# Eight experts of a group worked on from one on-chip set of token rows, selected and combined by one-hot matmuls

## The chip, the cores and the metric

The kernel runs on one core of a Trainium2 chip. The metric is the device time of one execution in microseconds (us); lower is better. TensorE is called PE here, VectorE DVE, ScalarE ACT, GpSimd POOL; SP is the sync engine, whose queue issues most of the transfers.

## The reference

One layer of a diffusion backbone over 1024 tokens of width 1024, all in fp32: a mixer (mLSTM and Hyena branches, merged), then a mixture of 64 experts in 8 groups of 8, then a final RMSNorm. Only the expert part bears on the change:

```python
glog = xt @ w_group + b_group                 # 8 groups, top 1
gsel = argmax(glog); gw = softmax(glog)[gsel]
elog = (xt @ w_router + b_router)[group gsel] # 8 experts of that group, top 2
weights = gw * topv / sum(topv)
expert(x) = (silu(x @ w1_e) * (x @ w3_e)) @ w2_e      # 1024 -> 512 -> 1024
h2 = rmsnorm(x, g_norm2) * (1 + mod4) + mod3
x = x + mod5 * sum over the two experts of weights * expert(h2)
out = rmsnorm(x, g_final)
```

Both experts of a token belong to one group. For the inputs used here the routing, worked out from the reference, gives 102 to 177 tokens to a group and at most 62 to an expert.

## The kernel before

The program is one long straight line per engine, put into order by a scheduler that sees all the dependences; within one engine instructions run in that order. The mixer takes the first 1590 us or so. Its last part (`merge`) writes each finished token row to a DRAM tensor `xg` (row and its 1/rms) and again to a DRAM tensor `xd`, the residual stream. `route` then ranks each token within its expert by matmuls with triangular ones and builds a table: 128 slots by 32 columns, column j holding 64 slots for expert j and 64 for expert j+32 (`idx` the token of a slot, `sw` its share). Slots that no token fills have an index out of bounds, and the gather skips them.

`experts` (line 1728) runs 32 iterations, j = 0 to 31, one pair of experts each. In iteration j:

- `gather` (line 1656) brings the 128 slot rows of iteration j+2 from `xg` into one of two `xs` buffers, by an indirect DMA on POOL's queue;
- `expert_up` (line 1681) multiplies `xT` with w1 and w3 of both experts: 32 matmuls of 64 columns by 512 rows, the two experts side by side in the PE array (column tiles 0 and 64), into two PSUM buffers `psz`; then silu on ACT and the product on DVE (`hm`);
- `prepare` (line 1661) makes `xT` of iteration j+1: eight 128x128 matmuls with the diagonal `dg` of 1/rms, which transpose and scale at once, and then the modulation, half on DVE and half on ACT;
- `expert_mid` (line 1695) transposes `hm` (four matmuls, line 1700) and copies the result to `hmT`;
- `expert_down` (line 1705) multiplies with w2 (16 matmuls), scales by share and `mod5` on DVE, and issues an indirect DMA that adds the 128 rows onto `xd` in DRAM.

An fp32 matmul is two instructions in the trace. PSUM holds three `psz` buffers and five `psx` buffers, taken in turn; a matmul into a `psx` buffer waits until the user of five allocations earlier is done.

The weights come through SP's queue in tiles of 1 MB (`wtile`, line 1625), 12 tiles for one pair, into a ring of NW = 19 buffers; a transfer waits for its buffer and for the fourth transfer before it. After j = 12 comes a loop (`more`, line 1799) for tokens beyond 64 of an expert; with these inputs it runs zero times, but the engines meet at its head. At the end `final_load` reads `xd` back, and `final` normalises and writes the output; the last pair's rows are added on chip and written after that (`renew`).

```python
for j in range(32):
    if j + 2 < 32:
        self.gather(xs[j % 2], ix[j + 2], P)
    ...
    hm = self.expert_up(mp, xT, W, P)
    if j < 31:
        xT = self.prepare(mp, xs[(j + 1) % 2], P)
    hT = self.expert_mid(mp, hm, P)
    ...
    add = self.expert_down(mp, hT, W, ix[j], sw[:, j:j + 1], P, acc=acc)
```

Of the kernel before, what the change touches and what calls it, by code (L numbers as in the profile page):

```python
# [9 lines left out]
F32 = mybir.dt.float32  # L10
# [27 lines left out]
NW, NA = 19, 12  # L38
# [60 lines left out]
class Body:  # L99
# [1162 lines left out]
    def merge_begin(self):  # L1262
# [3 lines left out]
        self.gp = self.kst.enter_context(self.pool("mgd", 3, side="right"))  # L1266
# [7 lines left out]
    def merge(self):  # L1274
        nc, I = self.nc, self.I
        mm = nc.tensor.matmul
        self.xd = self.dram.tile([S, D], F32, name="xd")
# [4 lines left out]
        with ExitStack() as st:  # L1282
# [6 lines left out]
            for half in range(2):  # L1289
# [41 lines left out]
                def post(t, c, ps):  # L1331
# [65 lines left out]
    def route(self, rt, hf):  # L1397

        nc = self.nc
# [6 lines left out]
        if hf == 0:  # L1406
# [5 lines left out]
            self.wt, self.rk, self.eid = kt("wt", 2, 8), kt("rk", 2, 8), kt("eid", 2, 8)  # L1412
            self.seen, self.tab0 = keep.tile([P, 64], F32R, name="seen"), kt("tab0", 96)
            ts(self.seen, self.iota[:, 0:64], 0.0, None, ALU.mult)
# [5 lines left out]
        def first_max(nm, v):  # L1420

            mx, oh, km = new(nm + "m", 4), new(nm + "o", 4, 8), new(nm + "k", 4)
# [5 lines left out]
            return mx, oh  # L1428

        gl = lg[:, :, 0:8]  # L1430
        gm, goh = first_max("g", gl)
# [6 lines left out]
        es = new("es", 4, 8)  # L1438
        red(es, sel)
        e1, oh1 = first_max("e1", es)  # L1440
        es2 = new("es2", 4, 8)
        stt(es2, oh1, -3.0e38, es, ALU.mult, ALU.add)
        e2, oh2 = first_max("e2", es2)

        f32r = lambda nm, *m: rt.tile([P, *m], F32R, name=nm)
# [4 lines left out]
        A = f32r("A", 4, 64)  # L1450
        tt(A, OH[:, 0], OH[:, 1], ALU.add)
# [3 lines left out]
        mm(pr[:, 0:256], self.sr[:, 1], self.seen.unsqueeze(1).broadcast_to([P, 4, 64]), start=True, stop=False)  # L1455
        mm(pr[:, 0:256], self.sr[:, 0], A, start=False, stop=False)
        for t in range(3):
            mm(pr[:, 64 * (t + 1):256], self.sr[:, 1], A[:, t:t + 1].broadcast_to([P, 3 - t, 64]), start=False,
               stop=(t == 2))
        odd, either, ohv = new("odd", 2, 4), new("either", 2, 4, 32), f32r("ohv", 2, 4, 32)  # L1460
        red(odd, OH[:, :, :, 32:64])
        for k in range(2):
            tt(either[:, k], OH[:, k, :, 0:32], OH[:, k, :, 32:64], ALU.add)
            tt(ohv[:, k], either[:, k], self.val[:, T].unsqueeze(2).broadcast_to([P, 4, 32]), ALU.mult)
        ohw = f32r("ohw", 2, 4, 2, 32)

        def weights():

            gw, r, w = new("gw", 4), new("r", 4), new("w", 4)
# [393 lines left out]
```

## Time and profile before

| | us |
|---|---|
| three runs, median (lowest to highest) | 2667.94 (2666.43 to 2678.24) |
| the profiled execution, its own time | 2671.49 |
| its span, first to last instruction | 2669.7 |
| PE busy (matmul) | 2486.4 (93%) |
| PE weight loads, beside the matmuls | 1675.9 (63%) |
| DVE busy | 1244.5 (47%) |
| ACT busy | 842.4 (32%) |
| mean granted PE clock | 0.971 |
| moved by DMA | 628.62 MB |

The profile shows one execution. The time of an execution is its span and 1.8 us around it. A row of the timeline is one or several instructions of one line in a row on one engine: start, length, engine, line, what it writes and reads, count, and in brackets how long the engine had waited and for what. PE is busy nearly everywhere, which by itself does not say that it sets the time; the windows and the timeline of the expert stage, from about 1625 us on, have to be read for that.

### The profile page before, as it was taken

How to read it: one execution, taken by the hardware profiler on the slowest of the kernel's cores; microseconds unless marked ns; L12 is line 12 of the kernel's file. 1: busy time of each engine (PE TensorE's matmuls, PEld its weight loads, DVE VectorE, ACT ScalarE, POOL GpSimd, SP SyncE). 2: the span in 40 equal slices, each digit the busy share in tenths (PEclk: the TensorE clock that was granted, in tenths of full speed). 3: DMA queues.
4: the chain of work that ended last, by engine and by line, in shares of the span. 5: the costliest groups of instructions: out<-in, count | busy, mean ns of one | idle time of the engine just before them, and what ended most of it. 6: DMA issues, size and time to landing. Idle time of an engine off the chain costs nothing. (4 is left out here: it accounts for less than half of the span.)

```text
span 2669.7 us, 31257 instructions
## 1 busy us (share of the span) xinstructions
PE 2486.4 (93%) x11726; PEld 1675.9 (63%) x11726; DVE 1244.5 (47%) x2845; ACT 842.4 (32%) x1606; POOL 212.5 (8%) x303
## 2 busy tenths in 40 slices
PE   7999999999999999999989997999888988898885
PEld 3777788888887888888868774444333333333332
DVE  5687868888842338766764533411111111111113
ACT  5454444554533346666343321100000000000001
POOL 1000000000010111011021010100000000000001
PEclk9999999999999999999999998999998999999997
DMA  7565532212252332233464579999998999999998
GB/s 270 157 192 159 167 126 73 73 57 81 72 148 65 110 83 84 67 99 119 161 220 148 169 245 373 412 405 400 407 403 335 412 405 394 396 396 397 401 406 330
DMA packets 236836, 628.62 MB, mean 235 GB/s; under 512 B 23514, under 2 KB 138696, under 8 KB 187532
## 3 DMA queue, kind: packets, MB, share of 16 engines
q1 hardware_dynamic: 195904, 522.49, 52.0%
q0 software_dynamic: 28800, 82.11, 9.8%
q10 hardware_dynamic: 11980, 22.01, 2.3%
q8 instruction: 93, 1.52, 0.2%
q14 instruction: 59, 0.48, 0.1%
HBM read 577.92 MB, written 65.68 MB: 241 GB/s over the span
## 5 line engine op out<-in xcount | busy, mean ns | idle before, releaser
L1688 PE MATMUL psz<-we,xT 128*64 128x512 f32 x2048 | 519.6, 618 | 56.0 <-DMA we<-in_w_e_dram 47.1
L1688 PEld LDWEIGHTS psz<-we,xT 128*64 128x64 f32 x2048 | 174.9, 142 | 354.8 <-issue 277.1
L1716 PE MATMUL psx<-we,hmT 128*64 128x512 f32 x1024 | 290.2, 614 | 24.1 <-issue 20.8
L107 DVE TENSOR_TENSOR hm<-hm,psz 128x512 f32<-128x512 f32 x32 | 22.0, 688 | 469.0 <-PE psz L1688 469.0
L122 ACT ACTIVATE xT<-psx,shp,gsp 128x128 f32<-128x128 f32 x128 | 55.4, 455 | 524.0 <-DVE xT L116 520.5
L697 PE MATMUL psz<-h0h,wh 128*128 128x512 f32 x512 | 204.0, 399 | 1.3 <-ACT h0h L122 1.3
L699 PE MATMUL psz<-h0h,wl 128*128 128x512 f32 x512 | 202.9, 396 | 0.8 <-DVE wl L535 0.8
L698 PE MATMUL psz<-h0l,wh 128*128 128x512 f32 x512 | 201.9, 394 | 0.6 <-DVE h0l L637 0.6
L699 PE MATMUL psz<-h1h,wl 128*128 128x512 f32 x512 | 201.0, 393 | 0.0
L697 PE MATMUL psz<-h1h,wh 128*128 128x512 f32 x512 | 200.5, 393 | 0.0
L698 PE MATMUL psz<-h1l,wh 128*128 128x512 f32 x512 | 200.3, 392 | 0.0
L1716 PEld LDWEIGHTS psx<-we,hmT 128*64 128x64 f32 x1024 | 88.7, 139 | 176.7 <-issue 166.0
L535 DVE TENSOR_TENSOR wl<-w,wh 128x1024 fp32r<-128x1024 f32 x104 | 127.0, 1222 | 148.4 <-ACT wh L534 124.4
L534 ACT CAST wh<-w 128x1024 fp32r<-128x1024 f32 x104 | 109.2, 1050 | 186.5 <-PE psz L698 167.2
L1670 PEld LDWEIGHTS psx<-dg,xs 128*128 128x128 f32 x512 | 124.9, 334 | 40.6 <-issue 34.8
L122 ACT ACTIVATE hm<-psz 128x512 f32<-128x512 f32 x32 | 19.1, 597 | 415.4 <-PE psz L1688 372.4
L1670 PE MATMUL psx<-dg,xs 128*128 128x128 f32 x512 | 132.2, 413 | 5.6 <-DVE dg L114 5.6
L116 DVE TENSOR_SCALAR xT<-psx,gsp,shp 128x128 f32<-128x128 f32 x128 | 49.8, 408 | 181.8 <-PE psx L1670 178.4
L110 DVE SCALAR_TENSOR_TENSOR yo<-psx,tab,m 128x512 f32<-128x512 f32 x64 | 48.0, 751 | 169.0 <-PE psx L1716 168.7
L697 PEld LDWEIGHTS psz<-h0h,wh 128*128 128x128 f32 x512 | 96.7, 189 | 26.5 <-issue 7.3
L699 PEld LDWEIGHTS psz<-h0h,wl 128*128 128x128 f32 x512 | 96.9, 189 | 23.8 <-issue 3.6
L698 PEld LDWEIGHTS psz<-h1l,wh 128*128 128x128 f32 x512 | 96.1, 188 | 22.1 <-issue 2.0
(570 smaller groups left out, 4665.4 us busy)
## 6 DMA issues: line engine op xcount, KB each, us to landing
we<-in_w_e_dram SPq DMA_DIRECT2D x366, 1024.0 KB
w<-in_w_in_dram SPq DMA_DIRECT2D x72, 512.0 KB
wm<-in_w_mod_dram SPq DMA_DIRECT2D x48, 512.0 KB
we<-in_w_e_dram SPq DMA_DIRECT2D x36, 512.0 KB
kd<-Ks ACTq DMA_DIRECT2D x8, 1088.0 KB
Kf<-kd SPq DMA_DIRECT2D x8, 1088.0 KB
gd<-sg ACTq DMA_DIRECT2D x32, 256.0 KB
w<-in_w_b_dram SPq DMA_DIRECT2D x16, 512.0 KB
```

What stands on the lines that cost most here:

```text
L107: (eng or self.nc.vector).tensor_tensor(out=out, in0=a, in1=b, op=op)
L110: self.nc.vector.scalar_tensor_tensor(out=out, in0=a, scalar=s, in1=b, op0=op0, op1=op1)
L116: self.nc.vector.tensor_scalar(out=out, in0=a, scalar1=s1, scalar2=s2, op0=op0, op1=op1)
L122: self.nc.scalar.activation(out=out, in_=in_, func=func, bias=bias, scale=scale, **kw)
L534: self.nc.scalar.copy(out=hi, in_=src)
L535: d = self.nc.vector.tensor_tensor(out=lo, in0=src, in1=hi, op=ALU.subtract)
L697: mm(ps, wh, xh, start=(k == 0), stop=False)
L698: mm(ps, wh, xl, start=False, stop=False)
L699: mm(ps, wl, xh, start=False, stop=(k == n - 1))
L1670: self.nc.tensor.matmul(pt[:, k * P:k * P + n], xs[:n, kk:D:8], dg[:n, :n], start=True, stop=True)
L1688: self.nc.tensor.matmul(ph[i][r, :], xT[:, k, r], w[i](k), start=(k == 0), stop=(k == 7), tile_position=(0, 64 * e))
L1716: nc.tensor.matmul(py[r, :], hT[:, k, r], w[2](k)[:, c * 512:(c + 1) * 512], start=(k == 0), stop=(k == 3), tile_position=(0, 64 * e))
```

## The change

The pair of iteration j becomes experts 2j and 2j+1, so that four iterations in a row (j = 4g to 4g+3) are the eight experts of group g. `route` ranks each token also within its group and builds a table of 256 rows for each group. `gather_group` fetches the rows of a group once, 2 x 128 of them, into `xs[g % 2]`; `normalize_group` scales them by 1/rms on ACT into `xn`. `prepare` picks the 128 slot rows of an iteration out of the group's 256 by a one-hot matrix `sel` in place of the diagonal: two matmuls (a = 0 and 1) where there was one. `expert_down` no longer adds to DRAM: the scaled result is split into `yh` and `yl` (fp32r), and `combine` adds it onto the group's rows on chip by one-hot matmuls, eight of 128x512 in each iteration, each result multiplied with `mod5` and added on DVE. After four iterations `finish` normalises the group's rows and writes them to the output by two indirect DMAs. `xd`, its copy in `merge`, the reading back at the end, `final` and `renew` go. The loop for the rest moves behind the last iteration; it takes tokens of a group beyond 256 or of an expert beyond 64, and has none with these inputs. The ring of weight buffers falls from 19 to 16, and a pool of gate tiles in `merge` from 3 to 2.

```diff
-NW, NA = 19, 12
+NW, NA = 16, 12
...
-        self.gp = self.kst.enter_context(self.pool("mgd", 3, side="right"))
+        self.gp = self.kst.enter_context(self.pool("mgd", 2, side="right"))
...
-                        nc.gpsimd.dma_start(self.xd[r, :], xv[:, t])
...
+        hi, row, g2 = new("hi", 4, tag="c4"), new("row", 4), new("g2", 4, 2, 8)
+        ts(hi, gr, 127.5, None, ALU.is_gt)
+        stt(row, hi, -128.0, gr, ALU.mult, ALU.add)
...
+        Rg = f32r("Rg", 4, P, tag="Rk")
+        tt(Rg, self.iota.unsqueeze(1).broadcast_to([P, 4, P]), row.unsqueeze(2).broadcast_to([P, 4, P]), ALU.is_equal)
...
+        for t in range(4):
+            mm(tgr, Rg[:, t], g3[:, t].rearrange("p a b -> p (a b)"), start=(t == 0), stop=(t == 3))
...
-        return self.wtile(("w1_e", "w3_e", "w2_e")[i // 2], j + 32 * (i % 2), first)
+        return self.wtile(("w1_e", "w3_e", "w2_e")[i // 2], 2 * j + i % 2, first)
...
+    def normalize_group(self, mp, g):
+
+        self.xn = mp.tile([P, 2, D], F32, name="xn")
+        for a in range(2):
+            x = self.xs[g % 2][:, a]
+            self.act(self.xn[:, a], x[:, :D], AF.Copy, scale=x[:, D:D + 1])
...
+    def prepare(self, mp, j):
+
+        g, p = divmod(j, 4)
+        sel = mp.tile([P, 2, P], F32, name="sel", bufs=2)
+        for a in range(2):
+            c = [self.cod[:, p, 16 * k + 8 * a + g:16 * k + 8 * a + g + 1] for k in range(2)]
+            self.ts(sel[:, a], self.iota, c[0], None, ALU.is_equal)
+            self.stt(sel[:, a], self.iota, c[1], sel[:, a], ALU.is_equal, ALU.add)
         xT = mp.tile([P, 8, P], F32, name="xT", bufs=2)
         for q in range(2):
             pt = self.ps()
             for k in range(4):
                 kk = 4 * q + k
-                self.nc.tensor.matmul(pt[:, k * P:k * P + n], xs[:n, kk:D:8], dg[:n, :n], start=True,
-                                      stop=True)
...
+                for a in range(2):
+                    self.nc.tensor.matmul(pt[:, k * P:(k + 1) * P], self.xn[:, a, kk:D:8], sel[:, a],
+                                          start=(a == 0), stop=(a == 1))
...
+    def combine(self, mp, j, y):
+
+        x = self.xs[j // 4 % 2]
+        st = mp.tile([P, 2, P], F32R, name="st", bufs=2)
+        for a in range(2):
+            self.ts(st[:, a], self.iota, self.row[:, a, j:j + 1], None, ALU.is_equal)
+        for a in range(2):
+            for c in range(2):
+                cs = slice(c * 512, (c + 1) * 512)
+                ps = self.ps()
+                for i in range(2):
+                    self.nc.tensor.matmul(ps, st[:, a], y[i][:, cs], start=(i == 0), stop=(i == 1))
+                self.tt(ps, ps, self.m5[:, cs], ALU.mult)
+                self.tt(x[:, a, cs], x[:, a, cs], ps, ALU.add)
+
+    def finish(self, mp, x, idx):
...
+        for a in range(n):
+            for c in range(2):
+                self.act(self.ps(), x[:, a, c * 512:(c + 1) * 512], AF.Square, accum_out=ss[:, a, c:c + 1])
+        self.tt(r, ss[:, :, 0], ss[:, :, 1], ALU.add)
+        self.rsqrt(mp, r, r, 1.0 / D)
+        for a in range(n):
+            self.stt(x[:, a, :D], x[:, a, :D], r[:, a:a + 1], self.gf, ALU.mult, ALU.mult)
+            off = bass.IndirectOffsetOnAxis(ap=idx[a], axis=0)
+            self.nc.gpsimd.indirect_dma_start(out=self.out[0], out_offset=off, in_=x[:, a, :D], in_offset=None, **OOB)
...
         for j in range(32):
-            if j + 2 < 32:
-                self.gather(xs[j % 2], ix[j + 2], P)
+            g, p = divmod(j, 4)
...
+            if p == 3 and g < 7:
+                self.normalize_group(mp, g + 1)
+            hm = self.expert_up(mp, xT, W)
+            if j > 0:
+                self.combine(mp, j - 1, y)
+                if p == 0:
+                    self.finish(mp, self.xs[(g - 1) % 2], group(g - 1))
+            if p == 0 and g < 7:
+                self.gather_group(g + 1)
             if j < 31:
-                xT = self.prepare(mp, xs[(j + 1) % 2], P)
...
+                xT = self.prepare(mp, j + 1)
+            hT = self.expert_mid(mp, hm)
+            y = [mp.tile([P, D], F32R, name=f"y{p}") for p in "hl"]
+            for c in range(2):
+                cs = slice(c * 512, (c + 1) * 512)
+                py = self.expert_down(hT, W, c)
+                self.act(y[0][:, cs], py, AF.Copy, scale=sw[:, j:j + 1])
+                self.stt(y[1][:, cs], py, sw[:, j:j + 1], y[0][:, cs], ALU.mult, ALU.subtract)
...
+        self.combine(mp, 31, y)
+        self.finish(mp, self.xs[1], group(7))
+        self.more(mp)
```

The scheduler puts the new work into an order of its own, which the diff does not tell. PE in a late iteration of the kernel before (`L1700` is `expert_mid`, `L1716` `expert_down`, `L1670` `prepare` for the next iteration, `L1688` `expert_up` of the next; counts are matmuls):

```order
L1700 MATMUL psx<-cmat,hm 128x128 x4
L1716 MATMUL psx<-we,hmT 64x512 x2
L1670 MATMUL psx<-dg,xs_14898 128x128 x8
L1716 MATMUL psx<-we,hmT 64x512 x14
L1688 MATMUL psz<-we,xT 64x512 x32
```

And in the changed kernel, within a group, from `expert_down` to the next `expert_up` (`L1760` is `expert_down`, `L1775` `combine`, `L1723` `prepare`, `L1737` `expert_up`):

```order
L1760 MATMUL psx<-we,hmT 64x512 x16
L1775 MATMUL psx<-yh,st 128x512
L1775 MATMUL psx<-yl,st 128x512
L1775 MATMUL psx<-yh,st 128x512
L1737 MATMUL psz<-we,xT 64x512
L1775 MATMUL psx<-yl,st 128x512
L1775 MATMUL psx<-yh,st 128x512
L1775 MATMUL psx<-yl,st 128x512
L1775 MATMUL psx<-yh,st 128x512
L1775 MATMUL psx<-yl,st 128x512
L1723 MATMUL psx<-sel,xn 128x128 x16
L1737 MATMUL psz<-we,xT 64x512 x31
```

The combine of an iteration stands right behind its own `expert_down`, and the prepare behind the combine, ahead of the next `expert_up` but for one matmul of it; in the kernel before, the prepare lay within `expert_down`.

At the six group boundaries j = 8, 12, ... 28 PE has one matmul of the prepare behind the combine, and the rest in the middle of `expert_up`:

```order
L1775 MATMUL psx<-yl,st 128x512
L1723 MATMUL psx<-sel,xn 128x128
L1737 MATMUL psz<-we,xT 64x512 x16
L1723 MATMUL psx<-sel,xn 128x128 x15
L1737 MATMUL psz<-we,xT 64x512 x15
```

DVE at such a boundary (`yl` is the low part of the result, `psx` times `m` and `xs` plus `psx` are the combine, from `r` on it is `finish`):

```order
L110 SCALAR_TENSOR_TENSOR yl<-psx,tab_13786,yh 128x512 x2
L107 TENSOR_TENSOR psx<-psx,m_15109 128x512
L107 TENSOR_TENSOR xs_14923<-xs_14923,psx 128x512
L107 TENSOR_TENSOR psx<-psx,m_15109 128x512 x2
L107 TENSOR_TENSOR xs_14923<-xs_14923,psx 128x512 x2
L107 TENSOR_TENSOR psx<-psx,m_15109 128x512
L114 TENSOR_SCALAR st<-cmat,rowt 128x128
L107 TENSOR_TENSOR xs_14923<-xs_14923,psx 128x512
L114 TENSOR_SCALAR st<-cmat,rowt 128x128
L107 TENSOR_TENSOR r<-ss 128x2
```

Four more `psx` buffers go to the squares of `finish` there, between those of the combine and those of the prepare, so that the prepare's first buffer is the one of the combine's fourth result.

## Rows read from the trace of the kernel before

**Rows 1.** The page, 40 slices of the span: PE busy, DMA share.
```profile
PE   7999999999999999999989997999888988898885
...
DMA  7565532212252332233464579999998999999998
```
**Rows 2.** Windows: PE, PEld, DVE, ACT, POOL busy (count), PE clock, DMA share, GB/s.
```profile
1700.00:1800.00 100.00, 95.66 (x408) 42.76 (x408) 17.90 (x40) 9.63 (x22) 9.29 (x8) 0.98 1.02 407
2200.00:2300.00 100.00, 88.80 (x359) 37.99 (x357) 13.88 (x27) 6.95 (x15) 7.88 (x6) 0.95 1.01 398
```
**Rows 3.** Timeline of PE, one iteration that waits for no weights (j = 5 to 6).
```profile
1786.16 0.75 PE L1700 MATMUL psx<-cmat,hm 128*128 128x128 f32 x4 [0.84 <-DVE hm L107]
1787.74 1.90 PE L1716 MATMUL psx<-we,hmT 128*64 128x512 f32 x4 [0.83 <-issue]
1789.58 4.08 PE L1670 MATMUL psx<-dg,xs 128*128 128x128 f32 x16
...
1800.13 14.27 PE L1688 MATMUL psz<-we,xT 128*64 128x512 f32 x61
1815.24 0.74 PE L1700 MATMUL psx<-cmat,hm 128*128 128x128 f32 x4 [0.84 <-DVE hm L107]
```
**Rows 4.** Timeline of PE, later: a wait for weights, and the last iterations.
```profile
1928.72 8.78 PE L1688 MATMUL psz<-we,xT 128*64 128x512 f32 x30 [3.07 <-DMA we<-in_w_e_dram]
...
2634.30 0.75 PE L1700 MATMUL psx<-cmat,hm 128*128 128x128 f32 x4 [0.85 <-DVE hm L107]
```
**Rows 5.** Timeline of PE, `expert_mid` of j = 0 and of j = 4.
```profile
1643.12 0.63 PE L1700 MATMUL psx<-cmat,hm 128*128 128x128 f32 x4
...
1756.13 0.75 PE L1700 MATMUL psx<-cmat,hm 128*128 128x128 f32 x4 [0.89 <-DVE hm L107]
```
**Rows 6.** DMA queues, 1700 to 2000 us: packets, MB, share of 16 engines.
```profile
q1 hardware_dynamic: 15932, 116.03, 94.3%
q0 software_dynamic: 2880, 5.10, 6.7%
```
**Rows 7.** Timeline of PE in the merge: fp32r matmuls of 128x512.
```profile
1542.29 0.40 PE L697 MATMUL psz<-wrh,Gh 128*128 128x512 f32 x1
...
1542.99 0.40 PE L697 MATMUL psz<-wrh,Gh 128*128 128x512 f32 x1
```
**Rows 8.** Groups of lines, 2200 to 2600 us: busy, mean ns | idle before.
```profile
L110 DVE SCALAR_TENSOR_TENSOR yo<-psx,tab,m 128x512 f32<-128x512 f32 x24 | 18.0, 751 | 58.9 <-PE psx L1716 58.9
...
L107 DVE TENSOR_TENSOR hm<-hm,psz 128x512 f32<-128x512 f32 x12 | 8.3, 688 | 192.7 <-PE psz L1688 192.7
L122 ACT ACTIVATE hm<-psz 128x512 f32<-128x512 f32 x12 | 7.2, 597 | 144.4 <-PE psz L1688 144.4
```
**Rows 9.** The start of the expert stage: timelines of POOL, DVE and PE.
```profile
1616.72 1.08 POOL L1658 DMA_INDIRECT xs<-xg,mgi  x1 [14.04 <-DVE tmp L1532]
...
1620.76 0.29 DVE L114 TENSOR_SCALAR dg<-cmat,xs 128x128 f32<-128x128 f32 x1 [2.78 <-DMA xs<-xg,mgi]
...
1621.11 4.21 PE L1670 MATMUL psx<-dg,xs 128*128 128x128 f32 x16 [5.59 <-DVE dg L114]
1625.24 14.01 PE L1688 MATMUL psz<-we,xT 128*64 128x512 f32 x64
```
**Rows 10.** The end: timelines of PE, ACT, DVE and POOL.
```profile
2635.83 7.14 PE L1716 MATMUL psx<-we,hmT 128*64 128x512 f32 x32 [0.79 <-DVE hmT L1702]
...
2642.18 1.28 ACT L122 ACT_TABLE_LOAD   x1
...
2650.49 1.06 ACT L122 ACTIVATE we<-we 128x1024 f32<-128x1024 f32 x1
...
2660.75 1.28 DVE L110 SCALAR_TENSOR_TENSOR we<-yo,r,we 128x1024 f32<-128x1024 f32 x1
...
2663.69 1.02 POOL L1797 DMA_INDIRECT out_dram<-we,mgi  x1 [23.21 <-DMA out_dram<-we]
```
**Rows 11.** Timeline of PE at the loop after j = 12.
```profile
2021.86 1.97 PE L1688 MATMUL psz<-we,xT 128*64 128x512 f32 x2 [8.83 <-issue]
```

More of the change, by code (lines that the diff above doesn't have):

```diff
@@ L1490, in route @@
+        rk = new("rk", 2, 4)
         red(rk, tmp)
[L1492 to L1503 removed]
@@ L1509, in route @@
+        rp, ohv = new("rp", 2, 4, tag="c8"), f32r("ohv", 2, 4, 32)
+        stt(rp, odd, 64.0, rk, ALU.mult, ALU.add)
+        stt(rp, ov.unsqueeze(1).broadcast_to([P, 2, 4]), 1000.0, rp, ALU.mult, ALU.add)
+        ts(gr, gr, 1.0, None, ALU.add)
+        for k in range(2):
+            tt(ohv[:, k], either[:, k], gr.unsqueeze(2).broadcast_to([P, 4, 32]), ALU.mult)
+        if hf == 1:
+            weights()
+        tv, tw = self.ps()[:, 0:32], self.ps()[:, 0:64]
         for k in range(2):
-            Rk = rt.tile([P, 4, P], F32R, name="Rk", bufs=1 + hf)
@@ new lines, in overflow @@
+        for t in range(8):
+            mm(pc[:, 0:8], self.sr[:, 1], A[:, t], start=(t == 0), stop=(t == 7))
+        cnt, thr, cmp, n, end, base, one = (new("cnt", 8), new("thr", 8), new("cmp", 8, 8), new("n", 8), new("end", 8),
+                                            new("base", 8), new("one", 8))
+        nc.vector.tensor_copy(out=cnt, in_=pc[:, 0:8])
+        ts(thr, self.iota[:, 0:8], 128.0, 0.5, ALU.mult, ALU.add)
+        over = lambda v, m: v.unsqueeze(2).broadcast_to([P, 8, m])
+        each = lambda v, m: v.unsqueeze(1).broadcast_to([P, 8, m])
@@ new lines, in overflow @@
+        nc.vector.tensor_copy(out=ex[:, 16:24], in_=end[:, 7:8].broadcast_to([P, 8]))
+        self.item = self.keep.tile([1, 24], I32, name="item")
+        nc.vector.tensor_copy(out=self.item, in_=ex[0:1, :])
+        rk, q, it = new("ork", 8), new("q", 8), new("it", 8)
+        tt(cmp, self.goh, pr[:, 0:64].rearrange("p (t g) -> p t g", g=8), ALU.mult)
+        red(rk, cmp)
+        ts(thr, thr, 127.0, None, ALU.add)
+        tt(cmp, over(rk, 8), each(thr, 8), ALU.is_gt)
+        red(q, cmp)
@@ new lines, in more @@
+            xT = mp.tile([P, 8, P], F32, name="xT", bufs=2)
+            for q in range(2):
+                pt = self.ps()
+                for k in range(4):
+                    nc.tensor.matmul(pt[:, k * P:(k + 1) * P], x[:, 0, 4 * q + k:D:8], dg, start=True, stop=True)
+                self.modulated(xT, q, pt)
+            for e in range(8):
+                W = [[self.wtile(nm, e0 + e) for nm in ("w1_e", "w3_e", "w2_e")]]
+                hT = self.expert_mid(mp, self.expert_up(mp, xT, W))
+                for c in range(2):
+                    cs = slice(c * 512, (c + 1) * 512)
+                    py = self.expert_down(hT, W, c)
+                    yo = mp.tile([P, 512], F32, name="yo", tag="yl")
+                    self.stt(yo, py, w[:, e:e + 1], self.m5[:, cs], ALU.mult, ALU.mult)
+                    self.tt(x[:, 0, cs], x[:, 0, cs], yo, ALU.add)
```

419 lines of the change are left out of this document (183 added, 236 removed).

## The prediction

> **What bounds the kernel now.** I read the page's slices first: from slice 25, about 1630 us on, the DMA row stands at 9 and PE at 8 or 9 [rows 1]. Both look full, so the windows come next: early in the expert stage PE is busy 95.7 of 100 us, later 88.8, while the DMA share is full in both [rows 2]. Then the timeline of PE tells what the two limits are. From j = 5 to j = 6 PE waits for no weights, and one iteration takes 1815.24 - 1786.16 = 29.08 us [rows 3]. Later it waits for weight tiles at the start of or within `expert_up` [rows 4]. From `expert_mid` of j = 4 at 1756.13 [rows 5] to that of j = 31 at 2634.30 [rows 4] lie 27 iterations in 878.2 us, 32.5 each. So the weight stream sets the pace, and PE alone would need 29.08: it has 3.4 us to spare in an iteration, no more. That is the number to hold against the change. The stream carries 12.58 MB for each pair of experts; POOL's own transfers, gathers and adds, take 6.7% of the engines beside the 94.3% of the weights [rows 6].
>
> **The change, part by part.** All times are of the profiled execution: span 2669.7, its own time 2671.49, 3.6 us above the median of the runs.
>
> *Removed from the DMA engines.* 2048 rows gathered, 2048 added (read and written), the copy `xd`, its reading back. What is left is 1024 rows gathered and 1024 written. POOL's share falls from 6.7% to a third or so. At 407 GB/s [rows 2] the weights of an iteration take 12.58 / 0.407 = 30.9 us, and about 0.26 MB of rows 0.6 more: an estimate of 31.5 us. This is worth about 1 us in an iteration while the stream sets the pace, and nothing once PE does.
>
> *Prepare, doubled.* Eight matmuls, 16 instructions, go from 1789.58 to the next start 4.0 us later (the row's length is 4.08 with the last one's drain) [rows 3], 0.25 us each. The change issues 32: +4.0 us on PE. It lay on PE's path before and does so now.
>
> *Combine, new.* Eight fp32r matmuls of 128x512. Three such follow each other in 1542.99 - 1542.29 = 0.70 us [rows 7], so 8 x 0.233 = 1.87 us.
>
> *A wait that the combine brings.* It stands right behind its own `expert_down` in PE's order, and its fourth matmul needs `yl` of the second half: 0.60 us on ACT (the silu row of the same shape) and 0.75 on DVE (the `yo` row) [rows 8], with handovers some 1.65 us after the last matmul of `expert_down`. Queued behind it are the rest of the combine, the prepare and all of the next `expert_up`. PE has three combine matmuls and one of `expert_up` to fill it: the third combine matmul can start at 0.85, ends at 1.1, and the lone `expert_up` matmul takes 0.9 (two take 1787.74 to 1789.58) [rows 3], to 2.0. The four of them would have cost 0.7 + 0.9 without the wait: 0.4 us lost. The bounds are 0 and 1.65; I take 0.4, which is built from the nearest rows.
>
> *The other waits* for `hm` (0.84) and `hmT` (0.83) [rows 3] stay. **The iteration becomes** 29.08 + 4.0 + 1.87 + 0.4 = 35.35 us on PE, above the 31.5 of the stream. PE is then the bound, and the weights are there: 16 buffers hold one and a third iterations, and a tile's buffer is free again nearly a whole iteration before its new content is used, so that the smaller ring costs nothing as long as PE is slower than the stream. Were it not, the ring's gaps would come on top of the 31.5.
>
> *Group boundaries.* At j = 8, 12, ... 28 the prepare's first matmul waits for the `psx` buffer of the combine's fourth result. DVE needs `yl` (done at 1.65) and then eight operations of 128x512 at 0.69 [rows 8]: 7.1 us behind `expert_down`, where PE would have been ready at 3.1. That is 4.0 us, six times: 24 us. Behind that matmul wait `expert_up` and all the rest. `finish` itself then runs on ACT, DVE and POOL beside `expert_up`, and the writes have a whole group's time. At j = 4 the order has half of `expert_up` ahead of this matmul, which covers it.
>
> *Small things at nothing.* `yl`, `st`, `sel` and the adds on DVE come to some 8 us more in an iteration in which DVE was busy under 5 of 32 [rows 2]. `normalize_group` is two ACT copies beside `expert_up`. The gate pool of two is covered by the 24 matmuls of a block (24 x 0.233 = 5.6 us) [rows 7]; were that too little, one DVE operation of 0.69 in some 30 blocks, 21 us.
>
> *The start.* Gather was issued at 1616.72, `expert_up` began at 1625.24 [rows 9]. Now the group's table takes about 1 us more of small DVE work, there are two gathers (1.08) and an ACT copy of 128x1024 (1.06), and the prepare costs another 4.2 [rows 9, 10]; the second prepare, ahead of `expert_mid` of j = 0, another 4.0. Together +11.4: `expert_mid` of j = 0 comes at 1643.12 + 11.4 = 1654.5 [rows 5].
>
> *The first four iterations* took 1756.13 - 1643.12 = 113.0 [rows 5]; `expert_up` and `expert_down` overlap there and cover the waits. With 4 x 5.87 they take 136.5: `expert_mid` of j = 4 at 1791.0.
>
> *j = 4 to 31:* 26 x 35.35 + 27.3 (the last has no prepare, 8.0 less) + 24 = 970.4: `expert_mid` of j = 31 at 2761.4. The meeting at the loop, 8.83 us of PE [rows 11], is gone from the middle; it was hidden in the mean of 32.5 above.
>
> *The end.* Before, 2669.7 - 2634.30 = 35.4 us. Now: `expert_mid` and `expert_down` 9.3 (0.75 + 0.8 + 7.7) [rows 4, 10]; to DVE's last add 7.1; a square on ACT 0.6 with its handover 0.3, a table load 1.28, seven small operations some 1.4, two scalings of 1.28: 13.2; the last indirect write, 6.0 from its issue to the end as before (2663.69 to 2669.7) [rows 10]; the loop's head, 8.83 less those 6.0, 2.8 [rows 11]. Together 31.3.
>
> **Sum:** 2761.4 + 31.3 = 2792.7 of span, and 1.8 around it: **2794 us**, 4.6% above the profiled execution, 4.7% above the median. This case's own range is 2771 to 2840: 0 to 1.65 for the wait in each of 27 iterations (-11 to +34), and half of the boundaries' 24 either way.
>
> **A rule weighed.** The 16 instructions of the prepare take 4.0 us, 0.25 each [rows 3]. The Trainium skill (TensorE: Matmul & The Clock Gate, Back-to-back issue gap) gives some 81 ns for a sustained matmul of 128 columns. By that the added half would cost 1.3 us and the sum would be lower by 31 x 2.7 = 84 us, an estimate of 2710. The row is of this very instruction in fp32, so it decides.
>
> **The rivals.**
> - *Cheaper prepares.* The added half might run into the time of the first half's weight loads. For it: four transposes of the same size take 0.60 to 0.63 us [rows 5], 0.15 each. Against it: the 16 stand at 0.25 each in every iteration. At 0.15 for the added ones 31 x 1.6 = 50 us less: **2745**.
> - *PSUM is emptied too slowly.* The boundary's wait could come in every iteration: each of the four combine results is read twice by DVE. Against it: within a group the prepare takes buffers that were left long before. For it: at six boundaries it must. Then 20 more iterations lose 4.0: **2874**. [...]
> - *The weights stay the bound (the other side).* If the added PE work fell into PE's waits, only the saved traffic would count: 878.2 x 0.943 = 828 for the weights and a third of POOL's share, 20, less the loop's 8.8: 839, so 39 less; +11 at the start, -4 at the end: **2639**. It decides below 839 / 27 = 31.1 us of PE in an iteration, that is if the additions cost 2.0 us and not 6.27. The prepare alone takes twice that.
> - *The parts cancel:* additions of about 3.4 us would fill the slack exactly, some **2670**. It would take prepares at half their price and a free combine.
>
> **How the numbers follow.** Forecast 0.72, PSUM in every iteration 0.12, cheaper prepares 0.05, the weights as bound 0.08, parts cancel 0.03. The range 2740 to 2874 takes in the first three and leaves out the last two. A measurement of this kernel can tell about 0.5%, 13 us, from no change. Faster 0.08, same 0.03, slower 0.89.
>
> **What would show it.** In the changed profile: `expert_mid` of one iteration to the next 35 us apart, 39 at the boundaries; 32 instructions of the prepare in 8.0 us; almost no PE wait for weights, and DMA windows below full; the granted clock near 1.00 throughout the stage. Wrong would be: an interval of 31 us with waits for weights (the stream still bounds), prepares of 5 us, or a wait for DVE ahead of the prepare in every iteration.

## The result and the profile after

| | before | after |
|---|---|---|
| median, us (four runs each) | 2669.61 | 2785.80 |
| lowest to highest | 2666.43 to 2678.24 | 2781.88 to 2788.81 |
| profiled execution: time, span | 2671.49, 2669.7 | 2784.48, 2782.7 |
| moved by POOL's own queue, MB | 82.11 | 65.03 |

The change makes the kernel slower: ratio 1.0429, 95% interval 1.0400 to 1.0458. The forecast was 2794.

The page of the changed kernel, slices, queues and two groups of instructions (busy, mean ns, idle before):

```profile
PE   7999999999999999999999969999999999999995
...
DMA  7555532121333223234734769989898988898982
...
q0 software_dynamic: 21776, 65.03, 7.1%
...
L1737 PE MATMUL psz<-we,xT 128*64 128x512 f32 x2048 | 482.4, 595 | 0.0
...
L1723 PE MATMUL psx<-sel,xn 128*128 128x128 f32 x1024 | 249.0, 401 | 13.3 <-DVE xs L107 9.9
```

The roles have changed hands [rows 1]. PE is at 9 through the expert stage, and it is DMA that drops, to 8 in many slices. `expert_up` (L1737) waits 0.0 us for anything, where it waited for weights before [rows 4]. The windows say it too, in the columns of [rows 2]: the DMA share falls below full.

```profile
2200.00:2300.00 100.00, 94.25 (x398) 48.38 (x395) 29.69 (x61) 13.88 (x24) 4.83 (x4) 0.98 0.89 360
```

One iteration on PE's timeline, against [rows 3]:

```profile
1827.77 0.75 PE L1748 MATMUL psx<-cmat,hm 128*128 128x128 f32 x4 [0.85 <-DVE hm L107]
1829.30 7.14 PE L1760 MATMUL psx<-we,hmT 128*64 128x512 f32 x32 [0.78 <-DVE hmT L1749]
1836.38 0.50 PE L1775 MATMUL psx<-yh,st 128*128 128x512 f32 x1
1837.17 0.50 PE L1775 MATMUL psx<-yl,st 128*128 128x512 f32 x1 [0.28 <-DVE yl L110]
...
1840.10 7.67 PE L1723 MATMUL psx<-sel,xn 128*128 128x128 f32 x32
1847.69 13.95 PE L1737 MATMUL psz<-we,xT 128*64 128x512 f32 x62
1862.49 0.75 PE L1748 MATMUL psx<-cmat,hm 128*128 128x128 f32 x4 [0.85 <-DVE hm L107]
```

From `expert_mid` to `expert_mid` it is 34.72 us; most intervals lie within 0.1 of 34.7. The prepare takes 1847.69 - 1840.10 = 7.59. At a group boundary (here j = 8) PE stands ahead of the prepare, and the interval is 37.11:

```profile
1905.81 0.50 PE L1775 MATMUL psx<-yh,st 128*128 128x512 f32 x1
...
1909.29 0.39 PE L1775 MATMUL psx<-yl,st 128*128 128x512 f32 x1
1911.33 0.74 PE L1723 MATMUL psx<-sel,xn 128*128 128x128 f32 x2 [1.65 <-DVE xs L107]
1912.00 7.09 PE L1737 MATMUL psz<-we,xT 128*64 128x512 f32 x32
```

Four intervals are some 1.7 us longer than their neighbours. Each has a stretch at a lower clock: `expert_down` takes 8.83 and not 7.14. The timeline, and the windows around it (PE busy, PE clock, DMA share, GB/s):

```profile
2146.35 8.83 PE L1760 MATMUL psx<-we,hmT 128*64 128x512 f32 x32 [0.78 <-DVE hmT L1749]
```
```profile
2110.00:2144.00 34.00, 32.78 (x140) 1.00 0.89 362
2144.00:2148.00 4.00, 2.40 (x10) 0.85 1.02 422
2148.00:2152.00 4.00, 4.00 (x15) 0.73 1.01 414
2152.00:2181.00 29.00, 28.09 (x120) 1.00 0.81 327
```

At the start DVE waits for a small DMA that the forecast did not have, and at the end the last scaling runs to 2765.0 (timeline of DVE). That DMA is issued by POOL, which at the end issues its second write late (timeline of POOL):

```profile
1610.66 0.61 DVE L107 TENSOR_TENSOR sel<-lg,goh 128x256 f32<-128x256 f32 x1 [5.67 <-DMA xg<-rb]
...
2762.51 2.48 DVE L110 SCALAR_TENSOR_TENSOR xs<-xs,r,gf 128x1024 f32<-128x1024 f32 x2
```
```profile
1603.77 0.77 POOL L1392 DMA_DIRECT2D xg<-rb  x1 [2.48 <-DVE rb L1391]
...
2764.07 1.77 POOL L1792 DMA_INDIRECT out_dram<-xs,mgi  x1 [122.91 <-DVE xs L110]
2769.62 0.97 POOL L1792 DMA_INDIRECT out_dram<-xs,mgi  x1 [3.78 <-issue]
```

### The profile page after: what moved, and what is told of

It reads as the page before. It is cut to its first block, busy times and chain, and to the rows that moved or that the text cites. A ratio compares the mean times of both kernels' runs of the same rounds, so it can differ in the third digit from the quotient of the medians.

```text
span 2782.7 us, 33165 instructions
## 1 busy us (share of the span) xinstructions
PE 2632.8 (95%) x12493; PEld 1823.7 (66%) x12493; DVE 1443.7 (52%) x3312; ACT 935.2 (34%) x1747; POOL 159.8 (6%) x254
## 3 DMA queue, kind: packets, MB, share of 16 engines
q0 software_dynamic: 21776, 65.03, 7.1%
## 5 line engine op out<-in xcount | busy, mean ns | idle before, releaser
L1737 PE MATMUL psz<-we,xT 128*64 128x512 f32 x2048 | 482.4, 595 | 0.0
L1737 PEld LDWEIGHTS psz<-we,xT 128*64 128x64 f32 x2048 | 150.8, 137 | 284.3 <-issue 278.2
L1723 PEld LDWEIGHTS psx<-sel,xn 128*128 128x128 f32 x1024 | 246.9, 334 | 24.4 <-DVE xs L107 12.5
L1723 PE MATMUL psx<-sel,xn 128*128 128x128 f32 x1024 | 249.0, 401 | 13.3 <-DVE xs L107 9.9
L1760 PE MATMUL psx<-we,hmT 128*64 128x512 f32 x1024 | 236.7, 611 | 22.8 <-DVE hmT L1749 22.0
L122 ACT ACTIVATE yh<-psx,tab 128x512 fp32r<-128x512 f32 x64 | 44.0, 687 | 444.7 <-PE psx L1760 441.9
L1760 PEld LDWEIGHTS psx<-we,hmT 128*64 128x64 f32 x1024 | 86.6, 139 | 150.8 <-issue 121.0
L110 DVE SCALAR_TENSOR_TENSOR yl<-psx,tab,yh 128x512 fp32r<-128x512 f32 x64 | 48.1, 751 | 232.1 <-ACT yh L122 229.6
```

What stands on the lines that cost most here:

```text
L110: self.nc.vector.scalar_tensor_tensor(out=out, in0=a, scalar=s, in1=b, op0=op0, op1=op1)
L122: self.nc.scalar.activation(out=out, in_=in_, func=func, bias=bias, scale=scale, **kw)
L1723: self.nc.tensor.matmul(pt[:, k * P:(k + 1) * P], self.xn[:, a, kk:D:8], sel[:, a], start=(a == 0), stop=(a == 1))
L1737: self.nc.tensor.matmul(ph[i][r, :], xT[:, k, r], w[i](k), start=(k == 0), stop=(k == 7), **kw)
L1760: self.nc.tensor.matmul(py[r, :], hT[:, k, r], w[2](k)[:, c * 512:(c + 1) * 512], start=(k == 0), stop=(k == 3), **kw)
```

## The experiments

The theory: an iteration lasts as long as the longer of two things, PE's instructions with its waits or the weight stream. The rivals: DVE empties PSUM too slowly; the smaller ring costs; PE's waits and not its instructions cost. All times are medians; the ratios are to the kernel before, run beside it on the same chip. Differences between runs set medians of different chips side by side; the kernel before took 2669.6 to 2673.6 us on them.

**1. Half of the prepare** (changed kernel; rows 128 to 255 of a group left out)

```diff
-                for a in range(2):
-                    self.nc.tensor.matmul(pt[:, k * P:(k + 1) * P], self.xn[:, a, kk:D:8], sel[:, a],
-                                          start=(a == 0), stop=(a == 1))
+                self.nc.tensor.matmul(pt[:, k * P:(k + 1) * P], self.xn[:, 0, kk:D:8], sel[:, 0],
+                                      start=True, stop=True)
```

> The second matmul of each pair in the prepare is gone (the rows 128 to 255 of a group's tile are left out of the expert inputs): 16 instructions fewer in each of 32 prepares, 0.237 us each by the changed kernel's own trace, 3.8 us. My theory (PE's own instructions set the 34.7 us of a regular iteration): PE alone falls to 30.9 us, just under the 31.5 that I estimated for the weight stream, so the stream takes over: waits for weights come back at expert_up, an iteration takes 31.5 to 32.0, and the time is about 2690 us (2665 if PE stays the bound at 30.9). Rival 1 (DVE empties PSUM too slowly): PE waits for DVE in place of the removed instructions, the gain stays below 30 us, 2756 or more. Rival 2 (the added matmuls were half hidden, as the cheaper prepares of the prediction): gain of 50 us, 2736.

Measured: 2660.70 us, ratio 0.9968 (0.9956 to 0.9979), 125 us below the changed kernel. PE's timeline, and a window of all engines:

```profile
1974.28 3.85 PE L1722 MATMUL psx<-sel,xn 128*128 128x128 f32 x16
1978.06 13.95 PE L1736 MATMUL psz<-we,xT 128*64 128x512 f32 x62
1992.86 0.75 PE L1747 MATMUL psx<-cmat,hm 128*128 128x128 f32 x4 [0.85 <-DVE hm L107]
```
```profile
2200.00:2300.00 100.00, 92.62 (x397) 41.58 (x398) 38.61 (x85) 20.65 (x38) 4.83 (x4) 1.00 1.00 409
```

An iteration takes 30.9 us, nearly all of them alike: 3.8 less, the price of 16 instructions in full. Both rivals fall. PE still sets the pace, with no wait for weights in its timeline, while the DMA share is at 1.00. With its boundary of 33.3 a group takes 31.5 in the mean, so the stream is no slower than my 31.5; whether it is faster, this run does not show. The doubled half of the prepare makes up the whole loss of the change.

**2. The combine without `yl`** (changed kernel; the low parts left out)

```diff
-                for i in range(2):
-                    self.nc.tensor.matmul(ps, st[:, a], y[i][:, cs], start=(i == 0), stop=(i == 1))
+                self.nc.tensor.matmul(ps, st[:, a], y[0][:, cs], start=True, stop=True)
...
-                self.stt(y[1][:, cs], py, sw[:, j:j + 1], y[0][:, cs], ALU.mult, ALU.subtract)
```

> The combine takes only the high part yh (yl and its four matmuls are left out, so the result has the lower precision of one rounded part). My theory: four matmuls of 0.233 us and the wait of 0.28 us for yl are gone, 1.2 us in 31 iterations, 37 us: about 2749 us. Rival 1 (what costs is the wait at the combine and not its matmuls): 0.3 us in an iteration, 2777 us. Rival 2 (DVE's work on PSUM sets the pace): DVE loses its two operations for yl, 2 x 0.75 us, and an iteration falls by 1.5 us or more, 2740 us, and a regular iteration shows waits for DVE ahead of the prepare in the kernel as it is, which I have not seen.

Measured: 2766.80 us, ratio 1.0362 (1.0345 to 1.0379), 19 us less and not 37. A regular interval falls to 33.84, by 0.87: four matmuls at 0.22. The wait stays: 0.34 us, now for `yh`. The intervals at the boundaries grew to 37.6 to 39.1, most of them 4.1 above their neighbours where it was 2.4, and took back part of the gain: each of the six has a stretch at a lower clock (0.96 over the interval of 37.97, 1.00 over its neighbours), which costs some 1.7 us; in the changed kernel one boundary has it. The price of the matmuls is confirmed; the wait as a price of `yl` is not.

**3. Twice DVE's multiplication out of PSUM** (changed kernel; the gate row counts twice)

```diff
                 self.tt(ps, ps, self.m5[:, cs], ALU.mult)
+                self.tt(ps, ps, self.m5[:, cs], ALU.mult)
```

> Each of the four combine results in PSUM is multiplied twice by the gate row (so the result is off by that factor): four more DVE operations of 128x512 on PSUM, about 0.69 us each, 2.8 us in an iteration. My theory: nothing in a regular iteration, since PE never waits for these buffers there; 2.8 us more at each of six group boundaries and at the end, some 20 us: about 2806 us. Rival (DVE's emptying of PSUM sets the pace, the rival of the prediction at 2874): 2.8 us in each of 31 iterations, 87 us: 2873 us.

Measured: 2773.81 us, ratio 1.0392 (1.0373 to 1.0411): 12 us faster, with 2.8 us more of DVE in each iteration. Regular intervals are the same 34.72, so the rival that DVE empties PSUM too slowly falls; the copy out of PSUM is not the bottleneck here. The Trainium skill (TensorEngine Tiling, PSUM Bottleneck) says that it may become one where tiling has made TensorE faster; here PE got more work. The gain has another source. In the scheduler's new order half of `expert_up` stands ahead of the prepare at the boundaries, where PE had waited:

```profile
2048.60 0.40 PE L1775 MATMUL psx<-yl,st 128*128 128x512 f32 x1
2048.93 7.09 PE L1737 MATMUL psz<-we,xT 128*64 128x512 f32 x32
2055.94 6.93 PE L1723 MATMUL psx<-sel,xn 128*128 128x128 f32 x28
```

**4. A ring of 14** (changed kernel)

```diff
-NW, NA = 16, 12
+NW, NA = 14, 12
```

> The ring of weight buffers goes from 16 to 14, nothing else. My theory: PE is the bound and the stream has some 3 us to spare in an iteration, so the time stays within 0.5% of 2786 us; the weight DMAs are issued later, and their share in the windows stays. Rival (the ring's loss from 19 to 16 is part of the loss of the change): two buffers fewer cost as much again or more, at least 15 to 30 us, 2800 to 2820 us, with waits for weight tiles ahead of expert_up or expert_down.

Measured: 2792.48 us, ratio 1.0454 (1.0436 to 1.0471), 0.24% above the changed kernel and within what I called the same. Regular intervals are 34.72 again. The step from 19 to 16 was not run by itself; but from 1800 us on the changed kernel's PE waits for no weight tile, so the ring is no part of the loss.

**5. The squares of `finish` out of PSUM** (changed kernel)

```diff
-                self.act(self.ps(), x[:, a, c * 512:(c + 1) * 512], AF.Square, accum_out=ss[:, a, c:c + 1])
+                self.act(self.sq, x[:, a, c * 512:(c + 1) * 512], AF.Square, accum_out=ss[:, a, c:c + 1])
...
+            self.sq = y[0][:, 0:512]
```

> The squares of finish are written into the buffer of yh, which is free then, and no longer into PSUM buffers; nothing else. My first reading of the group boundary was that the prepare there waits for PSUM buffers held by the combine's results and by these squares. If the squares are what holds them, the 2.4 us that an iteration takes longer at j = 8, 12 to 28 go: 6 x 2.4 = 14 us, about 2771 us. Rival: the prepare waits for the combine's own results, which DVE reads twice, or for the add to the tile that the next group's rows are taken from, and the squares have no part in it: 2786 us, with the same 37.1 us at the boundaries.

Measured: 2779.25 us, ratio 1.0407 (1.0388 to 1.0425). The boundary of j = 8 on PE's timeline, with no wait ahead of the prepare and the regular order:

```profile
1912.74 0.40 PE L1775 MATMUL psx<-yl,st 128*128 128x512 f32 x1
1912.97 7.67 PE L1723 MATMUL psx<-sel,xn 128*128 128x128 f32 x32
```

All the boundary intervals are 34.7 now but for stretches at a lower clock. So the squares caused the 2.4 us. They take four of the five PSUM buffers in turn, and by that order the prepare's first result falls on a buffer of the combine that DVE has not yet read. In the changed kernel PE's wait there ended, at 1911.33, with the third of DVE's four additions (DVE's timeline):

```profile
1910.00 1.28 DVE L107 TENSOR_TENSOR xs<-xs,psx 128x512 f32<-128x512 f32 x2
```

Only 6.5 us of 14 reached the total, and the single runs of the two kernels overlap (2775 to 2787 and 2782 to 2789). In the profiled execution eight intervals between j = 4 and 31 are 1.7 us longer, where four were: 7 us given back.

**6. `rb` in a tile that lives on** (changed kernel)

```diff
-                rb = tp.tile([P, 4, XW - D], F32, name="rb")
+                rb = self.wte[:, 4:8] if half else tp.tile([P, 4, XW - D], F32, name="rb")
```

> The tile rb of the second half lies in a tile that lives on (the one for the expert shares of the overflow, written later), so that the routing's tiles no longer lie on it and the first of them on DVE doesn't wait for rb's write to DRAM. My theory: the wait of 5.67 us on DVE at 1610.66 goes, expert_mid of j = 0 comes 5 to 6 us earlier, at about 1655, and the time is about 2780 us. Rival: behind it the gather waits for its own source rows, whose writes end at the same time, and the start stays: 2786 us.

Measured: 2784.49 us, ratio 1.0427 (1.0412 to 1.0441): no difference in the total that can be told. The wait itself is gone (DVE's timeline, then `lg`, the router's scores, in the changed kernel and in the kernel before):

```profile
1597.92 0.46 DVE L107 TENSOR_TENSOR lg<-lr,lc 128x288 f32<-128x288 f32 x1
...
1599.52 0.61 DVE L107 TENSOR_TENSOR sel<-lg,goh 128x256 f32<-128x256 f32 x1
```
```profile
1603.42 0.46 DVE L107 TENSOR_TENSOR lg<-lr,lc 128x288 f32<-128x288 f32 x1
1601.04 0.46 DVE L107 TENSOR_TENSOR lg<-lr,lc 128x288 f32<-128x288 f32 x1
```

From that `lg` to `expert_mid` of j = 0 it is 52.1 us, against 56.9 in the changed kernel: the mechanism held, 4.8 us. From j = 4 to 31 this execution has six stretches at a lower clock, against four, and takes 3.1 us more. Where `lg` stands differs by 13 us between the executions of the changed kernel and its variants (1597.9 to 1611.0), a spread in which 4.8 us cannot be told in the total.

**7. The kernel before without its scatter-adds** (31 of 32 left out)

```diff
-            if j < 31:
-                add()
```

> The kernel before without its scatter-adds of the expert results (31 of 32; the output lacks them): 128 rows of 4 KB read and written in each iteration. It prices the traffic that the change removes while the stream sets the pace. My theory (weights bound it, and POOL's transfers take a share of the same engines): some 0.7 to 1 us in an iteration, 2640 to 2650 us, and the interval falls from 32.5 to 31.5 or so. Rival (the adds cost nothing beside the weights, so the stream's pace is 32.5 in any case): 2670 us.

Measured: 2619.87 us, ratio 0.9818 (0.9800 to 0.9835): 51 us less, where I expected 20 to 30. The same windows as in [rows 2]:

```profile
1700.00:1800.00 100.00, 95.66 (x408) 42.59 (x407) 17.80 (x37) 8.79 (x19) 3.96 (x4) 1.00 1.01 419
2200.00:2300.00 100.00, 91.02 (x374) 38.46 (x376) 13.88 (x27) 6.96 (x15) 2.98 (x3) 0.97 1.01 417
```

The engines move 417 to 419 GB/s and not 398 to 407, and of that less is not weights. From j = 4 to 12 an iteration takes 29.07, PE's own pace; from j = 14 to 31, behind the loop, it is (2579.29 - 2054.67) / 17 = 30.9. The adds had cost 51 / 31 = 1.65 us in an iteration on average. From j = 14 to 30, where the stream is the bound in both kernels, it is 32.9 before and 30.9 here: 2.1.

**8. The kernel before with every prepare matmul issued twice**

```diff
-                self.nc.tensor.matmul(pt[:, k * P:k * P + n], xs[:n, kk:D:8], dg[:n, :n], start=True,
-                                      stop=True)
+                for _ in range(2):
+                    self.nc.tensor.matmul(pt[:, k * P:k * P + n], xs[:n, kk:D:8], dg[:n, :n], start=True,
+                                          stop=True)
```

> The kernel before with each matmul of the prepare issued twice with the same result: 16 more instructions in each iteration, and nothing else of the change. My theory: 4.0 us more on PE against a slack of 3.4 us, so PE alone needs 33.0 to 33.1 us and just passes the stream's 32.5; the first iterations, where PE is the bound already, take the whole 4 us. 5 iterations at +4.0 and 27 at +0.6, and the second prepare of the start: 2669 + 20 + 16 = about 2705 us. Rival 1 (the added half is hidden in weight loads of the first half at 0.15 us each): no more than 2.4 us in an iteration, 2682 us or less. Rival 2 (PE and the stream disturb each other, so that slack cannot be used): the whole 4 us every time, 2795 us.

Measured: 2734.87 us, ratio 1.0229 (1.0205 to 1.0252): 64 us more, between my 36 and the rival's 126. The regular interval is 33.26, 4.2 above 29.07 as expected. But about half of the intervals are 34.2 to 34.8, most with a stretch at the lower clock, so the mean from j = 4 to 31 is 34.0. PE waits for no weights from j = 4 on, so these stretches go into the total. The kernel before has 20 such stretches there beside 47 us of waits for weights; that they hide in time that the stream needs anyway was not tested.

**9. The prepare in fp32r parts, 10. PE's order, 11. all together** (changed kernel). Of 9, the core:

```diff
-                    self.nc.tensor.matmul(pt[:, k * P:(k + 1) * P], self.xn[:, a, kk:D:8], sel[:, a],
-                                          start=(a == 0), stop=(a == 1))
+                    for i in range(2):
+                        self.nc.tensor.matmul(pt[:, k * P:(k + 1) * P], self.xn[:, a, i, kk:D:8], sel[:, a],
+                                              start=(a == 0 and i == 0), stop=(a == 1 and i == 1))
```

> The prepare in another number form: a group's normalised rows are kept as a rounded high part and a low part in fp32r, the selection matrix in fp32r (zeros and ones), and each pair of fp32 matmuls becomes four fp32r matmuls. 32 instructions in a prepare as now, one weight buffer fewer (15) for the low part. Theory A (the 0.237 us of an instruction goes with the passes of its columns; an fp32r matmul of 128x512 took 0.233, so one of 128x128 about 0.06): the prepare falls from 7.6 to about 1.9 us, PE alone to 29.0 us, below the stream, which then sets the pace at 30.5 to 30.9 us (30.9 is what the runs so far still allow it): about 2670 us. Theory B (the price is that of an instruction with its own weight load of 128x128, whatever its form): 32 x 0.237 us stay, 2786 us.

Of 10, the core (the second half of the prepare is called behind `expert_mid`):

```diff
+                    if k == 0 and a == 0 and self.lastup is not None:
+                        self.after(d, self.lastmid if q else self.lastup)
```

> PE's order alone: the first half of the prepare is put between expert_up and expert_mid, the second half between expert_mid and expert_down, where PE waits 0.85 us for hm and 0.78 us for hmT in every iteration of the changed kernel. My theory (PE's instructions and its waits add up to the 34.7 us): both waits are filled, 1.6 us in an iteration, 50 us; and at the six group boundaries the prepare no longer stands ahead of expert_up, so the 2.4 us there go too, 14 us: about 2722 us. Rival 1 (the waits come back longer, since DVE now has the prepare's results to copy between hm and hmT): 2765 us or more. Rival 2 (the clock falls to half for 3.4 us more often the less PE waits, as with the kernel without the squares in PSUM, where it did so nine times and not four): 1.7 us in every third iteration, 17 us given back, 2740 us.

11 is 5, 6, 9 and 10 in one.

> All together: the prepare in fp32r parts, its two halves in PE's waits, the squares of finish out of PSUM, rb in a tile that lives on; 15 weight buffers. My theory: PE alone needs 27.5 to 29 us in an iteration, so the weight stream sets the pace, and without the scatter-adds at 30.5 to 30.9 us. From the run with half the prepare (2660.7 us, 30.9 in an iteration and 33.3 at the boundaries) less 6 x 2.4 us and the 5.7 us of the start: about 2640 us, 1% faster than the kernel before. Rival 1 (fp32r costs per instruction as fp32 does): PE needs 33.1 us, about 2722 us. Rival 2 (the stream with 15 buffers leaves gaps of its own, as the kernel before lost with 19 buffers at 32.5): 2665 to 2690 us.

Measured: 9 took 2834.84 us (1.0605, 1.0584 to 1.0625), 10 took 2717.96 (1.0171, 1.0152 to 1.0189), 11 took 2754.02 (1.0295, 1.0274 to 1.0315). Theory B of run 9 holds for the price of an instruction; the total is 49 us above its 2786. Undisturbed iterations take 34.95, and the rest lies in those with stretches at a lower clock: 26 from j = 4 to 31, some of them long, against four. Group of the prepare's weight loads and matmuls on the page of 9, to compare with L1723 above:

```profile
L1725 PEld LDWEIGHTS psx<-sel,xn 128*128 128x128 f32 x1024 | 251.1, 335 | 49.4 <-issue 33.3
...
L1725 PE MATMUL psx<-sel,xn 128*128 128x128 f32 x1024 | 256.4, 406 | 12.2 <-DVE xs L107 9.8
```

The fp32r instruction of 128x128 costs what the fp32 one does, and the loads of its 128x128 weights fill the slot: 251.1 / 1024 = 0.245 us each. That the load sets the price is an inference from these two rows. The Trainium skill (TensorE: Matmul & The Clock Gate, Back-to-back issue gap) says that load and matmul together set the spacing; its 81 ns is a third of what stands here. A rival is left: the prepare reads its weights with a stride of 8 elements, and such a load lasts 334 ns in run 10, where the combine's of 128x128, read without a stride, lasts 188. What the stride costs was not tested.

Run 10 fills both waits and removes the boundary's, as its timeline shows:

```profile
2012.50 4.07 PE L1724 MATMUL psx<-sel,xn 128*128 128x128 f32 x16
2016.41 0.63 PE L1752 MATMUL psx<-cmat,hm 128*128 128x128 f32 x4
2016.88 3.96 PE L1724 MATMUL psx<-sel,xn 128*128 128x128 f32 x16
2020.77 7.14 PE L1765 MATMUL psx<-we,hmT 128*64 128x512 f32 x32
```

Every interval from j = 5 to 30 is 33.0, 1.7 less than 34.7, with none at a lower clock: 68 us for an order. Run 11, with the fp32r prepare, has a stretch at the lower clock in every iteration, twice as long as those of the changed kernel, from the second half of the prepare into `expert_down`: 34.13 each, with no wait in front. Timeline, and windows of PE alone (busy, clock, DMA share, GB/s):

```profile
1999.87 4.07 PE L1726 MATMUL psx<-sel,xn 128*128 128x128 f32 x16
2003.86 8.71 PE L1767 MATMUL psx<-we,hmT 128*64 128x512 f32 x32
```
```profile
1997.00:2000.00 3.00, 3.00 (x16) 1.00 1.04 431
2000.00:2004.00 4.00, 4.00 (x19) 0.54 1.01 420
2004.00:2008.00 4.00, 4.00 (x12) 0.60 1.01 420
```

At a granted clock of 0.54 the 16 instructions of the prepare take 2003.86 - 1999.87 = 3.99 us, and at full clock in run 10 they took 2020.77 - 2016.88 = 3.89; `expert_down` goes from 7.14 to 8.71. The price of a prepare instruction hardly follows PE's clock, so something other than its columns sets it, as the inference has it.

**12. The old prepare with the new combine.** Each iteration gathers its 128 rows as before; the results are combined on chip. PE's order is that of 10, `rb` that of 6. Of the edit, the core:

```diff
+            if j + 2 < 32:
+                self.gather(self.xj[j % 2], self.xg, self.slots[:, j + 2:j + 3])
...
-                    self.nc.tensor.matmul(pt[:, k * P:(k + 1) * P], self.xn[:, a, kk:D:8], sel[:, a],
-                                          start=(a == 0), stop=(a == 1))
+                d = self.nc.tensor.matmul(pt[:, k * P:(k + 1) * P], x[:, kk:D:8], dg, start=True, stop=True)
```

> The prepare of the kernel before with the combine of the change: each iteration gathers the 128 rows of its pair of experts from DRAM and issues 16 instructions of the prepare, not 32; the results are combined into the group's tile on chip and written once, with no scatter-adds. The prepare's halves stand in PE's waits, as in the run with PE's order alone; rb lies in a tile that lives on. My theory (PE's instructions and the stream's pace, whichever is longer): PE alone 33.0 less 3.8 = 29.2 us, the stream without adds but with gathers 30.9, so 30.9 in an iteration: expert_mid of j = 0 at about 1650, 115 us for the first four, 27 x 30.9 = 834 and an end of 39 us, about 2640 us, 1% faster than the kernel before. Rival 1 (the gathers and not the adds slow the stream): 32.5 in an iteration, 2685 us. Rival 2 (with 16 buffers and not 19 the stream leaves gaps as soon as it is the bound): above 31.5 in an iteration with waits for weights, 2660 us or more.

Measured: 2634.38 us, ratio 0.9852 (0.9835 to 0.9868), faster than both kernels. PE's timeline and a window:

```profile
2154.06 8.78 PE L1741 MATMUL psz<-we,xT 128*64 128x512 f32 x30 [3.77 <-DMA we<-in_w_e_dram]
...
2191.99 2.18 PE L1726 MATMUL psx<-dg,xj 128*128 128x128 f32 x8
2194.00 0.63 PE L1753 MATMUL psx<-cmat,hm 128*128 128x128 f32 x4
2194.47 2.06 PE L1726 MATMUL psx<-dg,xj 128*128 128x128 f32 x8
```
```profile
2200.00:2300.00 100.00, 92.22 (x386) 40.30 (x385) 33.60 (x66) 17.00 (x32) 7.78 (x7) 0.98 1.01 415
```

From j = 4 to j = 9 the interval is 29.2, PE's own pace as worked out, with the prepare in PE's former waits; then the stream takes over at a share of 1.01, `expert_up` waits for weights again (2154.06), and the mean from j = 4 to 31 is 836.2 / 27 = 31.0. In that mean the first iterations run on tiles that had come ahead; from j = 14 to 30, where the stream is the bound, it is 31.7 at 416 GB/s, against 30.9 at 418 in run 7. So gathers are not what slowed the stream, the adds were, and 16 buffers carry the same rate; by time and rate run 12 moves 0.3 MB more in an iteration, an estimate, which accounts for the other 0.8 us.

## Why the prediction was right

The likeliest case came: PE became the bound, and its additions were priced from the rows. In the parts of its own sum:

| | forecast | measured |
|---|---|---|
| `expert_mid` of j = 0 | 1654.5 | 1660.3 |
| j = 0 to 4 | 136.5 | 132.8 |
| j = 4 to 31 | 970.4 | 950.8 |
| the end | 31.3 | 38.8 |
| span | 2792.7 | 2782.7 |

- *Prepare, doubled:* forecast +4.0, by the difference of the two traces +3.6 (7.59 less 4.0), by run 1 3.8. Right.
- *Combine and its wait:* forecast 1.87 + 0.4. From 1836.38 to 1840.10 less one us for the two `expert_up` matmuls within, 2.7 us: matmuls that follow another tile shape or a wait start 0.32 to 0.34 apart and not 0.233. The wait was at the second matmul, 0.28, not at the fourth. The rest of the iteration, unchanged in the forecast, became some 0.6 shorter. The rows point to `expert_down`: in the kernel before four of its instructions stand alone ahead of the prepare and take 1.84 us [rows 3], while in the changed one all 32 stand together and take 7.08, 0.22 each. That was not tested. So 34.71 for 35.35.
- *Group boundaries:* right in place and cause, mis-sized: 2.4 for 4.0. Run 5 bears out that the squares bring the prepare to a held buffer. But the forecast let PE wait for all eight operations of DVE, 7.1 behind `expert_down`, from 3.1 on; PE was ready at 3.9 and waited for six, until 5.5 (1911.33 - 1905.81): 1.65. The other 0.7 lies in PE's broken order there and was not looked into.
- *The ring and DVE at nothing:* held, by runs 3 and 4.
- *The stream:* 31.5 was never the bound here and so not measured: run 1, with the same transfers, moved them in 31.5 without a wait, which makes it an upper bound. Runs 7 and 12, with transfers of their own, took 30.9 and 31.7. The step that failed is the price of removed traffic, "about 1 us in an iteration" for adds, gathers and copies: the adds alone cost 1.65 to 2.1 by run 7. It counted bytes at an unchanged 407 GB/s, and the rate itself rose to 417. Nothing of it reached the total, since PE was the bound.
- *The other side:* the stream was to decide below 31.1 us of PE in an iteration. Run 1, at 31.5 with its boundaries, still waits for no weights and is level with the kernel before to 0.3%; run 12, at 29.2, does wait. Between the two nothing was run. The transfers of run 12 are not the change's.
- *The start:* 5.8 late. 2.4 of it lies ahead of `lg`, whose place differs by more than that between executions; before, it stood at 1601.04. From there to `expert_mid` it took 42.1 before and 56.9 now: 14.8 more, where 11.4 was forecast. The step lacked a wait: the routing's tiles lie on `rb`, whose DMA must end first (run 6: 4.8 us). Its other parts were forecast 1.4 too long.
- *The end:* 7.5 too short. It missed that the second indirect write waits behind the first on POOL: 2764.07 to 2769.62. From there to the end of the span it is 13.1 us, where 6.0 and 2.8 were counted. How these 13.1 divide between the write and the loop's head was not tried.
- *The clock:* four stretches, 1.7 us each, that the sum did not have.
- *A reading:* the rival of cheaper prepares took the four transposes at 0.60 to 0.63; [rows 5] has 0.63 and 0.75. Nothing else used it.

These errors cancel to 10 us; single terms were off by up to 20. The mechanism was right; that the total came within 8 us is in part luck.

## What to carry to other kernels

When two resources stand close, write down both paces, and price an edit on each: this change took 1.6 to 2.1 us an iteration from the stream that was the bound and put 5.6 on PE, which had 3.4 to spare. Look then at the parts one by one; the combine on chip pays, the selection by matmul doesn't, and keeping only the first, with PE's order changed as well, beat both kernels (that order was not tried on the kernel before by itself). Work that must be added to the bound engine should go first into the waits it already has: the same instructions in another order were worth 68 us.

## What the runs showed that was not expected

A 128x128 matmul instruction of the prepare took 0.24 to 0.25 us in fp32 and in fp32r alike (runs 9 to 11), in run 11 at the lower clock too, and one of 128x512 in fp32r took 0.233 [rows 7].

Stretches at the lower of TensorE's two clock levels (1.2 GHz and not 2.4) cost 1.7 us each in the changed kernel, as `expert_down` begins. There were four between j = 4 and 31, eight without the squares in PSUM, none in PE's other order, a longer one in every iteration with that order and fp32r in the prepare, and 26 with fp32r in the old order, many of them elsewhere in the iteration. What sets them off stays open: neither the waits ahead of `expert_down` nor their absence explains all of these.

POOL's scatter-adds, part of a queue that took 6.7% of the engines' time [rows 6], held the whole traffic at 398 to 407 GB/s; without them it ran at 417 to 419 (run 7).
